# An MLP block in fast matrix products: factors, copies, looks and sums of x take other engines and other places

## The chip, the cores and the metric

The kernel runs on one core of a Trainium2 chip. A core has five engines that work side by side, each through its own queue of instructions in order: TensorE (PE; its weight loads are PEld), VectorE (DVE), ScalarE (ACT), GpSimd (POOL) and SyncE (SP), which here only issues transfers. Sixteen DMA engines move data. The metric is device time in microseconds (us) of one execution.

## The reference

```python
def reference(x, w1, w2):          # x: 8 x 1024 x 1024, w1: 1024 x 4096, w2: 4096 x 1024
    h = x @ w1
    h = 0.5 * h * (1 + np.tanh(np.sqrt(2 / np.pi) * (h + 0.044715 * h ** 3)))
    return (h @ w2).astype(np.float32)
```

There are 8192 rows of x: two large products with a gelu between them.

## The kernel before, in words

Both products are done with fewer multiplications than the plain way. The first takes x and w1 as 2x2 blocks and forms seven products of sums of blocks instead of eight; the second uses a larger scheme of 26 products (`PRODUCTS`). The sums are made by VectorE in f16. To keep f16 in range, rows of x and column groups of w1 are scaled: a "look" finds the size of a tile, its reciprocal scales the cast to f16, and the factors `us` and `rs` undo and redo the scaling at the gelu.

**Tiles.** x comes in 64 chunks of 128 rows (`c`), two to an index `k` (32 of them). w1 is handled in four column groups `r`. A *unit* `u` is one pair (k, r), 128 in all, in the list `order`: first the six first k for r = 0 to 3 (24 units), then each middle k with its four r (a *quad* of units), then the last four k for each r. The first six units (`Plain`) use plain products, because the sums are not ready yet; the rest (`Quad1`) use the seven.

**A unit of Quad1.** `unit(u)` (L662) writes out, in order, m1 of the new unit, m7 of the unit before, the gelus g21 (of two units before) and g11, m3, m2, m6, the gelus g22 and g12, m5, m4, with slots 0 to 6 between them. m1, m6, m7 and m4 add to one PSUM bank `pa`; after m1 (L446), m6 (L456) and m7 (L465) ScalarE copies the bank out, and the next product into the same bank must wait for that copy. VectorE adds the other banks to these copies (L159). A gelu (L397) writes `e`, GpSimd scales and casts it to `g` (L168), and SyncE stores `g` in DRAM (`gd`, L402). Stores are held back a little by `let_go`.

**Order.** Nothing is scheduled automatically: each engine runs its instructions as they are written out. Side work is put into slots by `plan(u, slot, ...)`, `early(p, ...)` (step p of the first 24, four steps to a Plain unit) and done by `background`. Side work is: loading x (L177), the look (`look_x`, L181, a pass of ScalarE over the chunk that leaves a sum), `scale_x` (L184, L188, VectorE), the cast to f16 (L170), turning it (`turn_x_pe`: TensorE and a copy from PSUM, L213 on ScalarE or L215 on VectorE; later by a transposing DMA, L199), the four sums of x (`sum_x`, L159 and L162, tiles `xs`), the looks at w1 (L143), its scale (L262: `rows` on TensorE, L153, spreads the largest value), its casts and its sums (T1, T3, T2, T4), and, from about 390 to 660 us, loading, casting (`wu`) and summing (`wt`) w2, whose loads also go through SyncE's queue.

**Start.** Two chunks of x are loaded, looked at, cast and turned; a warm-up of 56 matmuls that compute nothing (L362) follows on TensorE, while VectorE takes the eight looks at w1. `factors(k, r)` (L229) makes `us` and its reciprocal `rs` with three VectorE instructions.

**Later x.** For a quad that starts at unit a, chunk h of x is loaded in slot 5 of unit a-7+h (L625), looked at in slot 5 of a-6+h (L626), cast in slot 4 and turned in slot 6 of a-5+h; its sums come in slot 5 of a-2 (L629).

Of the kernel before, what the change touches and what calls it, by code (L numbers as in the profile page):

```python
# [9 lines left out]
F16 = mybir.dt.float16  # L10
ACT = mybir.ActivationFunctionType
ALU = mybir.AluOpType
AX = mybir.AxisListType
P = 128
TINY = 1e-18
# [60 lines left out]
def kernel(  # L76
# [17 lines left out]
    HK = H // P // 2  # L94
    IK = I // P // 2
    NP = T // (2 * P)
    NR = I // 2 // N
# [8 lines left out]
    k4 = ctx.enter_context(tc.tile_pool(name="k4", bufs=15))  # L106
# [10 lines left out]
    xl = small.tile([P, T // P], F32, name="xl")  # L117
    xm = small.tile([P, T // P], F32, name="xm")
    xi = small.tile([P, T // P], F32, name="xi")
# [4 lines left out]
    w1m = small.tile([P, NR], F32, name="w1m")  # L124
    w1i = small.tile([P, NR], F32, name="w1i")
# [6 lines left out]
    us = small.tile([P, NP, 2, NR], F32, name="us")  # L132
    rs = small.tile([P, NP, 2, NR], F32, name="rs")
# [6 lines left out]
    V, S, G = nc.vector, nc.scalar, nc.gpsimd  # L140

    def absmax(dst, src):
        V.tensor_reduce(  # L143
            out=dst, in_=src, op=ALU.max, axis=AX.X, apply_absolute_value=True
        )
# [12 lines left out]
    def add(o, a, b):  # L158
        V.tensor_tensor(out=o, in0=a, in1=b, op=ALU.add)  # L159

    def sub(o, a, b):
        V.tensor_tensor(out=o, in0=a, in1=b, op=ALU.subtract)  # L162

    def cast(eng, o, i, s):
        if eng is S:
            S.activation(out=o, in_=i, func=ACT.Copy, scale=s)  # L166
        elif eng is G:
            G.tensor_scalar(out=o, in0=i, scalar1=s, scalar2=1.0, op0=ALU.mult, op1=ALU.mult)  # L168
        else:
            V.tensor_scalar(out=o, in0=i, scalar1=s, scalar2=None, op0=ALU.mult)  # L170


    xraw, x16, xT, xset = {}, {}, {}, {}

    def load_x(c, pool=k4, tag="k4"):
        xraw[c] = pool.tile([P, H], F32, name="xn", tag=tag)
        nc.sync.dma_start(out=xraw[c], in_=x2[c * P:(c + 1) * P, :])  # L177

    def look_x(c):
        junk = k2.tile([P, H], mybir.dt.bfloat16, name="junk", tag="k2")  # L180
        S.activation(out=junk, in_=xraw[c], func=ACT.Abs, accum_out=xl[:, c:c + 1])  # L181

    def scale_x(c):
        V.tensor_scalar(  # L184
            out=xm[:, c:c + 1], in0=xl[:, c:c + 1], scalar1=2.0 ** -13, scalar2=TINY,
            op0=ALU.mult, op1=ALU.max,
        )
        V.reciprocal(xi[:, c:c + 1], xm[:, c:c + 1])  # L188

    def cast_x(c, eng):  # L190
        scale_x(c)
        x16[c] = k2.tile([P, H], F16, name="x16", tag="k2")
        cast(eng, x16[c], xraw.pop(c), xi[:, c:c + 1])

# [19 lines left out]
        else:  # L214
            V.tensor_copy(out=xT[k][:, c % 2], in_=turned)  # L215

    def sum_x(k):
        t = xT[k]
        s = k4.tile([P, 4, HK, P], F16, name="xs", tag="k4")
        sums(s, t[:, 0, 0:HK], t[:, 0, HK:], t[:, 1, 0:HK], t[:, 1, HK:])  # L220
        xset[k] = s

    def sums(s, a11, a12, a21, a22):
        add(s[:, 1], a21, a22)
        sub(s[:, 2], s[:, 1], a11)
        sub(s[:, 3], a11, a21)
        sub(s[:, 0], a12, s[:, 2])

    def factors(k, r):  # L229
        at = slice(r, r + 1) if r is not None else slice(0, NR)  # L230
        for h in range(2):
            V.tensor_scalar(
                out=us[:, k, h, at], in0=w1m[:, at],
                scalar1=xm[:, 2 * k + h:2 * k + h + 1], scalar2=None, op0=ALU.mult,
            )
        V.reciprocal(rs[:, k, :, at], us[:, k, :, at])


    BLOCKS = (B11, B21, B12, B22)
# [3 lines left out]
    def load_w1(r, n, pool=wpool, tag="w"):  # L243
        b, half = BLOCKS[n // 2], n % 2
        row = (b in (B21, B22)) * HK * P + half * 2 * P
        col = (b in (B12, B22)) * I // 2 + r * N
        wraw[r, n] = pool.tile([P, 2, N], F32, name="wn", tag=tag)
        (G if r else nc.sync).dma_start(
            out=wraw[r, n],
            in_=w1[row:row + 2 * P, col:col + N].rearrange("(c p) n -> p c n", p=P),  # L250
        )

    def look_w1(r, n, keep):
        absmax(w1c[:, r, n:n + 1], wraw[r, n].rearrange("p c n -> p (c n)"))
        if not keep:
            wraw.pop((r, n))
# [10 lines left out]
    def cast_w1(r, n, eng):  # L267
        b, half = BLOCKS[n // 2], n % 2
        if (r, b) not in w1set:
            w1set[r, b] = wpool.tile([P, HK, N], F16, name="w", tag="w")  # L270
        cast(eng, w1set[r, b][:, 2 * half:2 * half + 2], wraw.pop((r, n)), w1i[:, r:r + 1])
# [87 lines left out]
    def warm_up(t, n):  # L359
        warm = bank("pb")  # L360
        for _ in range(n):
            nc.tensor.matmul(  # L362
                warm[:, :N // 2], lhsT=t[:, :P], rhs=t[:, :N // 2],
                start=True, stop=True, skip_group_check=True,
            )
# [196 lines left out]
    at = {}  # L562
# [5 lines left out]
    def plan(u, slot, f, *args):  # L568
        assert 0 <= u, (f, args)
        todo.setdefault((u, slot), []).append((f, args))  # L570

    def background(u, slot):
        for f, args in todo.pop((u, slot), ()):
            f(*args)


    def early(p, f, *args):
        plan(p // 4, p % 4, f, *args)

    for k in range(1, FIRST):  # L580
        for h in range(2):
            c = 2 * k + h
            if k > 1:
                p = (3, 7, 11, 14)[k - 2] + h
                early(p, look_x, c)
                early(p, cast_x, c, V)
            if k > 3:
                early((2, 5)[k - 4], load_x, c, wpool, "w")
            early(4 * k - 2 + 2 * h, turn_x_pe, c, V)
    for k in first:  # L590
        plan(*((4, 0), (4, 2), (5, 0), (5, 3), (FIRST, 3), (FIRST + 2, 3))[k], sum_x, k)
        for r in range(1, NR):
# [5 lines left out]
    early(16, widest_w1, 1)  # L598
    early(18, scale_w1, 1)
    for n in range(8):  # L600
        early(19 + n // 2, cast_w1, 1, n, (V, S, G, V, S, V, G, V)[n])
    for i, t in enumerate((T1, T3, T2, T4)):
        plan(5, (2, 3, 3, 3)[i], sum_w1, 1, t)
    for r in range(2, NR):
# [15 lines left out]
    for k in list(middle) + list(last):  # L620
        a = at[k] if k in middle else at[last[0]]
        for h in range(2):
            c = 2 * k + h
            late = 0 if k in middle else 2 * (k - last[0]) - 4
            plan(a - 7 + late + h if k in middle else a - 8 + late, 5, load_x, c)  # L625
            plan(a - 6 + late + h, 5, look_x, c)  # L626
            plan(a - 5 + late + h, 4, cast_x, c, V)
            plan(a - 5 + late + h, 6, turn_x, c, nc.sync)
        plan(a - 2 + late, 5, sum_x, k)  # L629
        plan(a - 2 + late, 4, factors, k, None)  # L630

    u = at[middle[0]] - 1
# [21 lines left out]
    for i, node in enumerate(FORMS):  # L654
        r, n = divmod(i, 7)
# [46 lines left out]
    with tc.manual_schedule(  # L702
        engines={
            mybir.EngineType.PE, mybir.EngineType.Activation, mybir.EngineType.DVE,
            mybir.EngineType.Pool, mybir.EngineType.SP,
        }
    ):
        for c in range(2):
            load_x(c, wpool, "w")
        for n in range(8):  # L710
            load_w1(0, n)
        V.memset(ones, 1.0)
        make_identity(nc, identity)
        V.tensor_copy(out=identity16, in_=identity)
        for c in range(2, 8):
            load_x(c, wpool, "w")
        for c in range(2):
            look_x(c)
            cast_x(c, S)
            t = x16[c]  # L720
            turn_x_pe(c, S)
        warm_up(t, WARM)
        for n in range(8):
            look_w1(0, n, True)
        widest_w1(0)
        scale_w1(0)
        warm_up(t, 16)
        for n in (0, 1, 2, 3, 4, 5):
            cast_w1(0, n, S if n in (2, 3) else V)
        factors(0, 0)  # L730
        for c in (2, 3):
            look_x(c)
        for c in (2, 3):
            cast_w1(0, c + 4, V)
            cast_x(c, V)
        factors(1, 0)
        for k in range(FIRST):
            if k > 1:
                factors(k, 0)
            Plain(k, 0).run(  # L740
                ("pa", "pc", "pa", "pc"),
                lambda i: [background(k, j) for j in ((i,) if i < 3 else (3, 4, 5, 6))],
            )
        now = {}
        for u in range(FIRST, NQ):
            unit(u, None)
        V.tensor_scalar(out=vo, in0=xm, scalar1=w2n, scalar2=None, op0=ALU.mult)
        V.tensor_scalar(out=vn, in0=vo, scalar1=-1.0, scalar2=None, op0=ALU.mult)
        for u in range(NQ, NQ + 2):
            unit(u, lambda i: second(3))  # L750
        let_go()
        for u in range(NQ + 2, NQ + 6):
            for slot in range(7):
                background(u, slot)
        assert not todo, todo.keys()
        second(NP * len(PRODUCTS) - done[0])
# [28 lines left out]
```

## Time and profile before

| what | value |
|---|---|
| median of 3 runs | 1564.81 us (1564.51 to 1565.39) |
| the profiled execution | 1567.52 us |
| its span in the profile | 1565.5 us |
| granted TensorE clock, mean | 0.998 |
| DMA share, 188 to 400 us | 0.80 |
| DMA share, 400 to 660 us | 0.91 |

By stretch, busy us of each engine (a Quad1 unit without pauses takes 6.04 us):

| stretch (us) | PE | DVE | ACT | POOL |
|---|---|---|---|---|
| 40 to 60 | 16.43 | 16.41 | 10.47 | 9.25 |
| 60 to 80 | 14.91 | 19.09 | 8.05 | 13.11 |
| 80 to 100 | 16.80 | 18.50 | 8.52 | 8.09 |
| 400 to 660 | 254.93 | 209.67 | 195.62 | 151.23 |
| 660 to 828 | 168.00 | 80.46 | 126.30 | 80.19 |

A busy engine isn't the limit by itself; what counts is who waited for whom in a stretch. The time in which TensorE pauses is what a change of side work can reach. In a row of the timeline stand the start, the time taken, the engine, the source line, the operation with its tiles (output before input) and shapes, how many, and in brackets the idle time before and what ended it.

### The profile page before, as it was taken

What the parts mean: (1) busy time and instruction counts of PE and PEld (TensorE: products, weight loads), DVE (VectorE), ACT (ScalarE), POOL (GpSimd) and SP (SyncE); (2) the same over time, 40 slices, a digit from 0 to 9 for tenths busy, and PEclk for the clock granted to TensorE, in tenths of its full rate; (3) what the DMA queues carried; (4) which work ended last, traced back from release to release, by engine and by line L of the source; (5) the groups of instructions that cost most, each with busy time, mean ns of one, the idle gap of its engine ahead of it and who ended that gap; (6) DMA issues with size and microseconds to landing.
All of it is one profiled execution on the core that took longest, in us unless ns stands there. A gap on an engine that the chain in (4) does not pass through costs nothing.

```text
span 1565.5 us, 28636 instructions
## 1 busy us (share of the span) xinstructions
PE 1527.2 (98%) x10437; PEld 1017.8 (65%) x10437; DVE 1189.7 (76%) x2422; ACT 724.5 (46%) x1280; POOL 443.9 (28%) x568
## 2 busy tenths in 40 slices
PE   7889999999999999999999999999999999999999
PEld 4334444444444444444446888888888888888888
DVE  5877766666777787856237888888888888888887
ACT  5457777777777777787663111111111111111111
POOL 2557644444555555655443000000000000000000
PEclk9999999999999999999999999999999999999999
DMA  8545687877899898894589776687677667766863
GB/s 309 168 138 188 183 243 236 245 233 214 250 263 271 235 275 234 276 256 141 184 217 283 140 149 134 123 162 136 137 134 155 138 125 151 143 134 128 162 134 83
DMA packets 459837, 293.92 MB, mean 188 GB/s; under 512 B 333872, under 2 KB 427056, under 8 KB 459696
## 3 DMA queue, kind: packets, MB, share of 16 engines
q1 hardware_dynamic: 456240, 279.52, 71.1%
q0 software_dynamic: 3456, 12.58, 2.5%
q8 instruction: 81, 1.33, 0.4%
q14 instruction: 60, 0.49, 0.1%
HBM read 96.99 MB, written 114.29 MB: 135 GB/s over the span
## 4 chain that ended last, share of the span: by engine, by line
PE 88%; DVE 4%; DMA 4%; ACT 2%; issue 1%; POOL 1%; SPq 0%; ACTq 0%; POOLq 0%; DVEq 0%
PE pa L350 47%; PE pc L350 28%; PE pb L350 13%; DMA wn<-in_w_dram 1%; DMA gd<-g 1%; DVE w1c L143 1%; DMA w<-wd 1%; DVE w L162 1%; ACT e L397 1%; DMA xn<-in_x_dram 1%; DVE e L159 0%; ACT junk L181 0%; DVE xs L162 0%; POOL g L168 0%; ACT w L166 0%
## 5 line engine op out<-in xcount | busy, mean ns | idle before, releaser
L168 POOL TENSOR_SCALAR g<-e,rs 128x512 f16<-128x512 f32 x512 | 396.6, 786 | 372.6 <-ACT e L397 238.3
L350 PEld LDWEIGHTS <-gs 128*128 128x128 f16 x4608 | 450.6, 98 | 55.8 <-DVE gs L162 1.6
L350 PEld LDWEIGHTS <-xs 128*128 128x128 f16 x1952 | 191.1, 98 | 248.0 <-DVE w L162 11.2
L159 DVE TENSOR_TENSOR e<-pc,e 128x512 f32<-128x512 f32 x244 | 160.9, 685 | 194.8 <-ACT e L465 194.3
L350 PEld LDWEIGHTS <-xT 128*128 128x128 f16 x1656 | 161.4, 98 | 198.3 <-DVE xT L215 5.1
L350 PE MATMUL pa<-w,gs 128*128 128x256 f16 x2304 | 288.3, 273 | 1.6 <-ACT e L397 1.0
L350 PE MATMUL pa<-w,xs 128*128 128x512 f16 x976 | 251.3, 380 | 14.7 <-DVE w L162 9.7
L397 ACT ACTIVATE e<-e,us 128x512 f32<-128x512 f32 x366 | 252.8, 722 | 20.1 <-DVE e L159 19.6
L350 PE MATMUL pa<-w,xT 128*128 128x512 f16 x1072 | 253.9, 379 | 4.0 <-DVE xT L215 3.1
L350 PE MATMUL pc<-w,xs 128*128 128x512 f16 x976 | 251.4, 380 | 0.8 <-DVE e L159 0.8
L350 PEld LDWEIGHTS <-gT 128*128 128x128 f16 x2048 | 200.3, 98 | 24.2 <-DMA w<-wd 1.1
L519 ACT ACTIVATE o<-pa,vo 128x256 f32<-128x256 f32 x96 | 45.4, 473 | 335.7 <-PE pa L350 333.3
L350 PE MATMUL pc<-w,gs 128*128 128x256 f16 x1536 | 193.8, 273 | 0.0
L350 PE MATMUL pa<-w,gT 128*128 128x256 f16 x1024 | 132.7, 273 | 0.8 <-DMA w<-wd 0.8
L350 PE MATMUL pb<-w,xT 128*128 128x512 f16 x488 | 125.2, 379 | 0.0
L515 DVE SCALAR_TENSOR_TENSOR o<-pc,vo,o 128x256 f32<-128x256 f32 x160 | 77.1, 482 | 58.4 <-PE pc L350 58.4
L456 ACT COPY e<-pa 128x512 f32<-128x512 f32 x122 | 71.6, 587 | 93.9 <-PE pa L350 89.0
L162 DVE TENSOR_TENSOR gs<-gT,gs 128x1024 f16<-128x1024 f16 x160 | 109.9, 687 | 0.7 <-POOL g L168 0.5
L515 DVE SCALAR_TENSOR_TENSOR o<-pa,vo,o 128x256 f32<-128x256 f32 x192 | 92.4, 481 | 20.1 <-PE pa L350 20.1
L350 PE MATMUL pb<-w,gs 128*128 128x256 f16 x768 | 99.5, 273 | 0.3 <-DMA gd<-g 0.3
L350 PE MATMUL pc<-w,gT 128*128 128x256 f16 x768 | 99.5, 273 | 0.0
L446 ACT COPY e<-pa 128x512 f32<-128x512 f32 x122 | 70.6, 579 | 47.5 <-PE pa L350 47.5
(82 smaller groups left out, 1362.4 us busy)
## 6 DMA issues: line engine op xcount, KB each, us to landing
gd<-g SPq DMA_DIRECT2D x488, 128.0 KB, 2.8
wn<-in_w_dram SPq DMA_DIRECT2D x72, 512.0 KB, 4.7
xn<-in_x_dram SPq DMA_DIRECT2D x64, 512.0 KB, 4.7
out_dram<-o SPq DMA_DIRECT2D x62, 512.0 KB, 3.7
w<-wd SPq DMA_DIRECT2D x25, 512.0 KB, 5.9
wn<-in_w_dram POOLq DMA_DIRECT2D x24, 512.0 KB, 5.4
wd<-wt SPq DMA_DIRECT2D x24, 512.0 KB, 4.4
gd<-g SPq DMA_DIRECT2D x12, 256.0 KB, 4.5
```

The lines of the kernel that those rows point to most:

```text
L143: V.tensor_reduce(out=dst, in_=src, op=ALU.max, axis=AX.X, apply_absolute_value=True)
L159: V.tensor_tensor(out=o, in0=a, in1=b, op=ALU.add)
L162: V.tensor_tensor(out=o, in0=a, in1=b, op=ALU.subtract)
L168: G.tensor_scalar(out=o, in0=i, scalar1=s, scalar2=1.0, op0=ALU.mult, op1=ALU.mult)
L350: nc.tensor.matmul(bank, lhsT=left(i), rhs=right[i], start=start and i == 0, stop=i == n - 1, skip_group_check=True,)
L397: S.activation(out=e, in_=src, func=ACT.Gelu_apprx_tanh, scale=self.u[half])
L446: S.copy(self.e11, self.pa)
L456: S.copy(self.e12, self.pa)
L515: V.scalar_tensor_tensor(out=o, in0=ps, scalar=v, in1=o, op0=ALU.mult, op1=ALU.add)
L519: S.activation(out=o, in_=ps, func=ACT.Copy, scale=v)
```

## The change

1. `factors` goes to GpSimd: for one r, two instructions of 128x2 (`us` = xm times w1m, `rs` = xi times w1i, with no reciprocal); for all r, four of 128x4. In the first units they are written a step after the cast of x.
2. Copies of the turned x for the first half of k = 2 to 5 go from VectorE to ScalarE; the casts of w1's second group (r = 1) are dealt out anew, with one more on ScalarE and one less on VectorE.
3. At the start, three of the eight looks at w1 stand ahead of the second `scale_x` on VectorE.
4. `scale_x` is planned by itself; for middle and last quads the look at x moves from slot 5 to slot 3 of the same unit, the scale stands in slot 4 of the next, before the cast as it did.
5. The four sums of x of those quads go to slots 5 and 6 of unit a-2 and slots 1 and 3 of unit a-1.

```diff
     def cast_x(c, eng):
-        scale_x(c)
         x16[c] = k2.tile([P, H], F16, name="x16", tag="k2")
...
+    def times(o, a, s):
+        G.tensor_scalar(out=o, in0=a, scalar1=s, scalar2=1.0, op0=ALU.mult, op1=ALU.mult)
 
     def factors(k, r):
-        at = slice(r, r + 1) if r is not None else slice(0, NR)
-        for h in range(2):
-            V.tensor_scalar(
-                out=us[:, k, h, at], in0=w1m[:, at],
-                scalar1=xm[:, 2 * k + h:2 * k + h + 1], scalar2=None, op0=ALU.mult,
-            )
-        V.reciprocal(rs[:, k, :, at], us[:, k, :, at])
+        if r is not None:
+            c = slice(2 * k, 2 * k + 2)
+            times(us[:, k, :, r], xm[:, c], w1m[:, r:r + 1])
+            times(rs[:, k, :, r], xi[:, c], w1i[:, r:r + 1])
+        else:
+            for h in range(2):
+                c = 2 * k + h
+                times(us[:, k, h, :], w1m, xm[:, c:c + 1])
+                times(rs[:, k, h, :], w1i, xi[:, c:c + 1])
...
                 early(p, look_x, c)
+                early(p, scale_x, c)
                 early(p, cast_x, c, V)
+                if h:
+                    early(p + 1, factors, k, 0)
...
-            early(4 * k - 2 + 2 * h, turn_x_pe, c, V)
+            early(4 * k - 2 + 2 * h, turn_x_pe, c, V if h or k == 1 else S)
...
-        early(19 + n // 2, cast_w1, 1, n, (V, S, G, V, S, V, G, V)[n])
+        early(19 + n // 2, cast_w1, 1, n, (S, V, G, S, V, S, G, V)[n])
...
-            plan(a - 6 + late + h, 5, look_x, c)
+            plan(a - 6 + late + h, 3, look_x, c)
+            plan(a - 5 + late + h, 4, scale_x, c)
             plan(a - 5 + late + h, 4, cast_x, c, V)
             plan(a - 5 + late + h, 6, turn_x, c, nc.sync)
-        plan(a - 2 + late, 5, sum_x, k)
+        for i in range(4):
+            plan(*((a - 2 + late, 5), (a - 2 + late, 6), (a - 1 + late, 1), (a - 1 + late, 3))[i], sum_x, k, (i,))
         plan(a - 2 + late, 4, factors, k, None)
...
         for c in range(2):
             look_x(c)
+            if c:
+                for n in range(3):
+                    look_w1(0, n, True)
+            scale_x(c)
             cast_x(c, S)
...
         warm_up(t, WARM)
-        for n in range(8):
+        for n in range(3, 8):
             look_w1(0, n, True)
```

`sum_x(k, parts)` now makes the sums named in `parts`. TensorE's and SyncE's queues hold the same instructions in the same order as before.

## The prediction

> **What bounds the kernel now.** The page's busy times come first: TensorE is the engine to fill.
>
> ```profile
> PE 1527.2 (98%) x10437; PEld 1017.8 (65%) x10437; DVE 1189.7 (76%) x2422; ACT 724.5 (46%) x1280; POOL 443.9 (28%) x568
> ```
>
> From 165 to 435 us, from 620 to 825 and from 860 on its matmuls follow each other without a pause, so nothing can be won there; only its pauses elsewhere can be. The table of who waited for whom, for TensorE over the whole span, names them:
>
> ```profile
> PE pa L350 <- DVE w L162: 9.7, 3, 6.2
> PE pa L350 <- ACT e L446: 5.0, 8, 1.2
> PE pa L350 <- DVE xT L215: 3.1, 3, 1.4
> PE rows L153 <- DVE spread L148: 1.8, 2, 1.6
> ```
>
> The three of VectorE lie in the first 161 us. The longest (6.2 us) is where the plain products end: the first quad's matmul with T2 waits for the sums of w1, and the chain of waits shows VectorE working without a break in front of it:
>
> ```profile
> 77.87 1.13 DVE w L162
> 79.00 0.76 DVE xs L159
> ...
> 80.88 2.28 DVE w L162 x2
> ...
> 83.20 1.89 PE pa L350 x4
> ```
>
> The granted clock stands at 0.50 from 80.0 to 86.8 in the windows of this stretch, so the first 8 matmuls after it run at half speed and lose another 1.7 us. The waits for ACT e L446 lie elsewhere: six of the eight, 4.2 us, between 400 and 660, where w2 is cast and summed. One of them, at the timeline's 557 us:
>
> ```profile
> 551.11 0.45 SPq L177 DMA_DIRECT2D xn<-in_x_dram  x1
> 551.72 0.59 ACT L456 COPY e<-pa 128x512 f32<-128x512 f32 x1 [0.38 <-PE pa L350]
> 554.11 1.03 PE L350 MATMUL pa<-w,xs 128*128 128x512 f16 x4
> 556.08 1.06 ACT L181 ACTIVATE junk<-xn 128x1024 bf16<-128x1024 f32 x1 [2.54 <-DMA xn<-in_x_dram]
> 557.14 0.57 ACT L446 COPY e<-pa 128x512 f32<-128x512 f32 x1
> 557.76 1.02 PE L350 MATMUL pa<-w,xs 128*128 128x512 f16 x4 [0.89 <-ACT e L446]
> ```
>
> ScalarE reaches the look at x (L181) 2.5 us before x has landed and stands. Behind it on its queue is the copy of a bank (L446) that TensorE must have before it adds to that bank again. That is the case to learn from, because the change moves this look.
>
> **Part 1, the first looks at w1 (L720 to L728).** Three of eight looks go ahead of the second `scale_x`, into 4.4 us in which VectorE idles. Tiles 0, 1, 2 of w1 land at 7.1, 8.5 and 9.8 us, so the looks run 7.1 to 11.0; the second `scale_x`, ready at 10.5, starts at 11.0. The eighth look then ends near 17.8 rather than 19.8 (its tile lands at 16.6). But these two lines stand between it and the end:
>
> ```profile
> 12.87 7.39 PE L362 MATMUL pb<-x 128*128 128x256 f16 x56
> 20.47 0.30 PE L153 MATMUL rows<-identity,spread 128*128 128x128 f32 x1 [0.21 <-DVE spread L148]
> ```
>
> The warm-up's 56 matmuls are ahead of `rows` on TensorE; they now start 0.6 us later (x is scaled later) and take the same time, so `rows` comes at about 20.7 to 20.8 instead of 20.47. The 2 us are lost behind the warm-up, which is not shortened. **+0.3** (0 to +0.6).
>
> **Part 2, VectorE relieved up to 83 us (factors L229, copies L215, casts L601).** It loses five pairs of factors (0.5 us each: two L232, one L236), four copies of the turned x (0.68 each; on ScalarE a copy is 1.01, L213) and one cast of w1 (0.75): 2.5 + 2.7 + 0.75 = 6.0 us. I walked VectorE's new order with these rows. Up to 60 us each copy of a quad's second half still stands behind a cast that waits for a look on ScalarE, so TensorE's four pauses there shrink from 1.5, 1.5, 1.1 and 0.6 to 1.0, 1.0, 0 and about 1.6: 1.0 won. The moved copies end before TensorE needs them (the first runs 36.4 to 37.4, wanted at 37.7). The spread is ready at 64.1 (65.7 now), w1's reciprocal at 66.3 (68.4 now). Then come sums of x (16 instructions of 0.42, in this stretch 0.42 to 0.72 on average per form), two casts and the sums of w1 at 1.2: T2 is ready at 76.9 with no delays, near 79.4 with the 2.5 us by which the same instructions stretch now beside GpSimd. Taken: 79.5 instead of 83.2, **-3.7** (-2.8 to -5.7), since the rows show the stretching. The half clock costs 1.7 now; the pause falls from 6.2 to about 4.4 us, and pauses of 2.5 us (at 120) did not lower the clock, so I take half: **-0.8** (0 to -1.7).
> The Trainium skill (TensorE: Matmul & The Clock Gate, Part 1) puts the gate's window at about 3.4 us, free-running; by it a pause of 4.4 us may or may not hold one idle window. The granted clock of this trace (64.85 us high, 6.83 low, multiples of 3.41) agrees.
>
> **Part 3, factors on GpSimd (48 instructions of 128x2, 104 of 128x4).** No such instruction is in the trace. Bounds: below 0.10 (its memset of 128x1), above 0.69 (cast of 128x512); the two casts, 0.69 and 1.12 for 512 and 1024 columns, leave 0.27 at no columns, which I take. A pair is 0.54. In units 17 and 23 it stands ahead of GpSimd's last cast of w1 (118.11 and 156.03), for which T3 on VectorE waits: +0.5 at 119; at 156 VectorE starts 0.5 earlier, about 0. **+0.5** (0 to +1.2). Elsewhere GpSimd idles enough (it is 47% busy from 200 to 400): the four of a quad, 1.1 us, hold the next casts of g and the stores behind these on SyncE once in 24 us, and `us` is due two units later.
> [...]
>
> **Part 4, the look at x in slot 3 (L626).** Its load stays in slot 5 of the unit before. In ScalarE's new order the look stands ahead of the unit's copy L456, which TensorE's m7 (L462) waits for, and of two gelus, not behind them. That undoes the pauses in which gelus held the look and the look held L446 (0.45, 0.8, 0.7, 1.05 and 1.3 us at 439, 506, 513, 557 and 614), and about 1.0 of those that wait for VectorE: **-5.3** (-3 to -6.2). Against it stands the load:
>
> ```profile
> DMA to landing us min/median/max: 3.7/3.9/5.4
> ...
> DMA to landing us min/median/max: 4.3/4.8/7.3
> ```
>
> These are x's loads from 200 to 400 and from 425 to 660. In the first stretch nearly all land 0.5 to 1.7 us before the unit's copy L456 starts, and the look slips into ScalarE's 0.8 us of idleness: no loss. In the second, stores that wait for GpSimd hold SyncE's queue, and the landings of the 20 loads lie after the start of that copy by 2.5, 1.6, 0.9, -0.4, 2.7, 2.7, 3.2, 1.6, 1.3, 2.1, 4.3, 0.4, 1.6, 1.7, 2.4, 3.4, 1.2, 2.7, 2.1 and -0.6 us. The copy then starts 1.04 after the landing (556.08 to 557.14). TensorE wants its bank 2.35 us after the copy's usual start (551.72 to 554.11) and can go on 0.62 after the copy's start (557.14 to 557.76), so 1.7 us are free; the pause is landing + 1.04 - 1.72. The same sum for L446 at 557 gives 1.05, as measured. A quad's second load is issued before the first look's pause shows, so that pause is taken off it. Sum: 18.6 us, and 1.0 for the load at 164.2 (1.7 late). Longer units give the DMA engines (0.91 busy from 400 to 660, 0.80 from 200 to 400) more time: at 7% slower their share is 0.86, half way back to 3.9, and the loads of w2 that hold SyncE shorten too. About a third off: **+13** (+3 to +19.6).
>
> **Part 5, sums spread.** The 104 sums of 26 quads keep their number; the last two of four move up to a unit on, and the quad that reads them starts after that: nothing, hidden under the unit's 6.0 us of products; without that cover 0.42 for each late one.
>
> **Sum.** +0.3 - 3.7 - 0.8 + 0.5 - 5.3 + 13 = **+4.0**. The profiled execution took 1567.5 us (its span 1565.5 and 2.0 around), 2.7 over the median of 1564.8; I carry the difference over: 1568.8 by the median.
>
> **Rivals.**
> *The loads come in time* (0.21): SyncE's stores wait for GpSimd's casts, and these for loads of w2; if TensorE's first pauses let that queue clear, later loads land within 0.7 us of the copy and cost nothing. It decides where the landing moves 2 us forward. For it: lateness does not grow along the list. Against: each load of w2 starts the delay afresh. Part 4's 13 falls to 3: -6.0, 1558.8, faster.
> *Half cleared* (0.18): part 4 at 9: 0.0, 1564.8, no change.
> *Nothing cleared, little won early* (0.11): 19.6 in part 4, part 2 at -2.8 and the gate still falling, -4.3 won: +13.3, 1578.
> *The looks don't do what they say*: that the order of w1's looks brings nothing is in the forecast; had the warm-up room, it were -2, inside the range.
> *GpSimd holds VectorE* (0.05): with a sum of 0.42 going to 0.80 at each of some 12 factor instructions up to 83 us, 4.5 us of part 2 are gone: +8.5, 1573.3.
>
> **How the numbers follow.** The forecast has 0.45, from 1566 to 1574. 0.2% is 3.1 us, about what a measurement here tells from no change. Faster: the first rival's 0.20. Same: the second, and 0.07 from the edges of the others, 0.25. Slower: 0.55. The range 1558 to 1577 leaves out some of the third rival and of the first.
>
> **What would show it.** Right: after, L465 copies (the old L456) between 430 and 660 start 1 us after a look whose gap names DMA xn, and TensorE's matmuls on pa wait for that copy, ten times and more; no wait for the copy of m1 there; `rows` at 20.7; TensorE's pause near 77 to 80 us at 3 to 5 us. Wrong: if looks there show no gap for DMA xn, the load came earlier than I think, and the time falls below 1562; if the clock stays at 1.00 and T2 is ready by 77.5, part 2 was worth 7.

## The result, and the profile after

| | us |
|---|---|
| before, median of 5 runs on the same chip | 1565.39 (1564.51 to 1566.96) |
| changed, median of 5 runs | 1580.68 (1579.04 to 1583.88) |
| ratio | 1.0098, 95% interval 1.0084 to 1.0113 |
| profiled execution of the changed kernel | 1581.5, its span 1579.7 (before: 1567.5, 1565.5) |

The change costs 15.3 us (1%), where the prediction had 4.0, and the time lies 3.7 us above its range. The changed file's lines that come up again: L359 is the product (L350 before), L455 the copy of m1 (L446), L465 the copy of m6 (L456), L406 the gelu (L397), L233 the new `times` on GpSimd.

The busy times and TensorE's table of waits in the changed kernel's profile (microseconds in total, times, longest):

```profile
PE 1532.4 (97%) x10437; PEld 1019.2 (65%) x10437; DVE 1165.7 (74%) x2267; ACT 728.6 (46%) x1285; POOL 481.4 (30%) x720
...
PE pa L359 <- ACT e L465: 13.3, 12, 2.4
...
PE pa L359 <- DVE w L162: 9.9, 3, 5.9
PE pb L359 <- DVE gs L162: 2.5, 1, 2.5
```

VectorE is busy 24 us less and GpSimd 37.5 us more, as the diff says; neither is where the time went. The table has a new first line: twelve waits for ScalarE's copy of m6, 13.3 us, where the kernel before had 5.0 us for the copy of m1. The waits for the sums of w1 (9.9 us; 9.7 before) have not shrunk, although VectorE was relieved ahead of them.

What the looks at x (L181) wait for from 165 to 700 us, first before, then changed (microseconds, times):

```profile
  DMA xn<-in_x_dram: 5.2, 5
```

```profile
  DMA xn<-in_x_dram: 34.4, 19
```

ScalarE stood five times in front of a late x, now it stands nineteen times. One of them, in the changed kernel's timeline (start, length, engine, line, and in brackets the idle time before and what ended it):

```profile
553.50 0.75 SPq L177 DMA_DIRECT2D xn<-in_x_dram  x1
...
555.65 1.89 PE L359 MATMUL pa<-w,xT 128*128 128x512 f16 x8
...
558.26 1.06 ACT L181 ACTIVATE junk<-xn 128x1024 bf16<-128x1024 f32 x1 [3.74 <-DMA xn<-in_x_dram]
559.22 0.19 ACT L181 ACTIVATION_READ_ACCUMULATOR junk<-xn 128x1 f32 x1
559.31 0.57 ACT L465 COPY e<-pa 128x512 f32<-128x512 f32 x1
...
559.93 1.02 PE L359 MATMUL pa<-w,xs 128*128 128x512 f16 x4 [2.39 <-ACT e L465]
```

The load is issued at 553.50 and lands some 4.7 us later; the look that waits for it holds ScalarE for 3.74 us; the copy behind it starts 1.05 after the landing (558.26 to 559.31), and TensorE goes on 0.62 after that. These are the steps that the prediction gave, at the same durations (1.04 and 0.62).

To find where the 15 us came from, I took the start of each matmul in the trace, less the start of the one before and the usual distance for its shape, and added up what is left over, half clock included. It gives 35.3 us before and 50.0 after, 14.7 more; the spans differ by 14.2. By stage, with a second profile of the same changed kernel (the last experiment) beside it:

| stage | before | changed | second profile | difference | predicted |
|---|---|---|---|---|---|
| up to 112 us: warm-up, T2's pause, half clock | 20.7 | 20.9 | 20.5 | +0.1, -0.2 | -4.2 |
| 112 to 165 us: later sums of w1 | 4.9 | 5.4 | 5.4 | +0.5, +0.5 | +0.5 |
| 165 to 665 us: looks at x while w2 is cast | 6.2 | 13.4 | 18.5 | +7.2, +12.3 | +7.7 |
| 665 to 700 us: a look at 685, half clock after | 0 | 4.2 | 4.4 | +4.2, +4.4 | 0 |
| from 820 us | 3.5 | 6.2 | 3.9 | +2.7, +0.4 | 0 |

The second profile runs some 5 us behind the first at 660 us; its pause at 666.4 us is the one that the first has at 661.4 and is counted in the same row.

So the prediction's main term has the right mechanism, and in the first profile about the right size (4.6 us more in the second). What failed in both is the start, where 4.2 us were to be won and nothing was, and one late look at 685 us that was not in the sum. The 2.7 us of the last row belong to the first profile alone.

### The profile page after: what moved, and what is told of

Read it like the earlier page. It is cut to its first block, busy times and chain, and to the rows that moved or that the text cites. A ratio compares the mean times of both kernels' runs of the same rounds, so it can differ in the third digit from the quotient of the medians.

```text
span 1579.7 us, 28618 instructions
## 1 busy us (share of the span) xinstructions
PE 1532.4 (97%) x10437; PEld 1019.2 (65%) x10437; DVE 1165.7 (74%) x2267; ACT 728.6 (46%) x1285; POOL 481.4 (30%) x720
## 4 chain that ended last, share of the span: by engine, by line
PE 60%; DMA 2%; ACT 1%; issue 0%; SPq 0%; DVE 0%; POOL 0%; ACTq 0%; POOLq 0%
PE pa L359 31%; PE pc L359 20%; PE pb L359 9%; DMA xn<-in_x_dram 1%; DMA w<-wd 1%; DMA gd<-g 1%; ACT e L465 0%; ACT junk L181 0%; SPq L353 0%; ACT e L406 0%; DVE gs L162 0%; POOL g L168 0%; ACT e L455 0%; DVE o L524 0%; SPq L411 0%
## 5 line engine op out<-in xcount | busy, mean ns | idle before, releaser
L168 POOL TENSOR_SCALAR g<-e,rs 128x512 f16<-128x512 f32 x512 | 386.7, 765 | 337.6 <-ACT e L406 246.1
L359 PEld LDWEIGHTS <-gs 128*128 128x128 f16 x4608 | 450.8, 98 | 56.6 <-DVE gs L162 2.8
L359 PEld LDWEIGHTS <-xs 128*128 128x128 f16 x1952 | 191.7, 98 | 260.3 <-issue 24.5
L359 PEld LDWEIGHTS <-xT 128*128 128x128 f16 x1656 | 161.8, 98 | 197.8 <-DVE xm L184 2.9
L359 PE MATMUL pa<-w,gs 128*128 128x256 f16 x2304 | 288.4, 273 | 0.0
L359 PE MATMUL pa<-w,xs 128*128 128x512 f16 x976 | 253.0, 382 | 24.2 <-ACT e L465 13.3
L359 PE MATMUL pa<-w,xT 128*128 128x512 f16 x1072 | 254.6, 380 | 3.1 <-DVE xm L184 1.9
L406 ACT ACTIVATE e<-e,us 128x512 f32<-128x512 f32 x366 | 252.3, 721 | 9.2 <-DVE e L159 8.8
L359 PE MATMUL pc<-w,xs 128*128 128x512 f16 x976 | 253.1, 382 | 0.0
L359 PEld LDWEIGHTS <-gT 128*128 128x128 f16 x2048 | 200.2, 98 | 24.9 <-DMA w<-wd 1.8
L359 PE MATMUL pc<-w,gs 128*128 128x256 f16 x1536 | 193.8, 273 | 0.2 <-DMA w<-wd 0.2
L359 PE MATMUL pa<-w,gT 128*128 128x256 f16 x1024 | 132.7, 273 | 1.0 <-DMA w<-wd 1.0
L359 PE MATMUL pb<-w,xT 128*128 128x512 f16 x488 | 125.5, 380 | 0.0
L524 DVE SCALAR_TENSOR_TENSOR o<-pa,vo,o 128x256 f32<-128x256 f32 x192 | 92.1, 480 | 19.8 <-PE pa L359 19.4
L359 PE MATMUL pb<-w,gs 128*128 128x256 f16 x768 | 99.5, 273 | 2.5 <-DVE gs L162 2.5
L455 ACT COPY e<-pa 128x512 f32<-128x512 f32 x122 | 71.0, 582 | 66.3 <-PE pa L359 66.0
L465 ACT COPY e<-pa 128x512 f32<-128x512 f32 x122 | 70.7, 580 | 63.8 <-PE pa L359 57.8
L359 PE MATMUL pc<-w,gT 128*128 128x256 f16 x768 | 99.5, 273 | 0.0
```

Of the source, the lines that this page charges most:

```text
L359: nc.tensor.matmul(bank, lhsT=left(i), rhs=right[i], start=start and i == 0, stop=i == n - 1, skip_group_check=True,)
L406: S.activation(out=e, in_=src, func=ACT.Gelu_apprx_tanh, scale=self.u[half])
L455: S.copy(self.e11, self.pa)
L465: S.copy(self.e12, self.pa)
L524: V.scalar_tensor_tensor(out=o, in0=ps, scalar=v, in1=o, op0=ALU.mult, op1=ALU.add)
```

## Experiments

Ratios are to the kernel before on the same chip, with their 95% interval. "Early" in a label means x loaded one unit sooner.

**The look back in slot 5.**

```
-            plan(a - 6 + late + h, 3, look_x, c)
+            plan(a - 6 + late + h, 5, look_x, c)
```

> The changed kernel with only the look at x put back into slot 5 of its unit; all other parts of the change stay. If the look in slot 3 holds the copy e (L465) for an x that has not landed, the pauses 'PE pa L359 <- ACT e L465' (13.3 us, 12 waits) go, the smaller pauses of the kernel before return between 430 and 660 us (about 6 us in place of 13.4), and the 3.9 us at 685 go too: 1580.7 - 7 - 4 = about 1570, and 1567.5 if the pause at 842 was a consequence as well. The rival, that factors on GpSimd or the spread sums cost the time, expects the pauses to stay under other names: 1577 or more.

Measured: 1564.26 us, 0.999 (0.998 to 1.000). All of the loss is gone with this one number. It came out below the 1567.5 to 1570 that I expected: between 165 and 700 us only 2.7 us of pauses are back, not 6. With 6.5 after 820 (eight matmuls at half clock among them) the rest adds up to about that of the kernel before (6.2 and 3.5). The rest of the change (GpSimd's factors, copies on ScalarE, first looks, spread sums) is together worth nothing that can be told from no change.

**Only the look, on the kernel before.** The same line of the kernel before, from 5 to 3.

> The kernel before with only the look at x moved from slot 5 to slot 3. The theory of the late load expects its cost alone: 7 to 11 us over the kernel before, about 1575, with ten or more waits of TensorE for the copy e behind a look that waits for DMA xn between 430 and 690 us. The rival (the loss needs the factors on GpSimd or the spread sums) expects no more than 2 us over the kernel before.

Measured: 1576.08 us, 1.0057 (1.0040 to 1.0074), 9 us slower. Its table of waits has the changed kernel's line:

```profile
PE pa L350 <- ACT e L456: 12.7, 12, 2.1
```

Twelve waits, 12.7 us, with nothing else of the change in the kernel: the look's slot alone makes them. The pause at 685 us (2.31 us) is there as well. The 9 us are what I expected (7 to 11).

**The load a unit earlier, the look in slot 3.**

```
-            plan(a - 7 + late + h if k in middle else a - 8 + late, 5, load_x, c)
+            plan(a - 8 + late + h if k in middle else a - 8 + late, 5, load_x, c)
```

> The changed kernel with the loads of x of the middle quads planned one unit (6 us) earlier, the look still in slot 3. The theory of the late load expects no look between 430 and 660 us to wait for DMA xn by more than 1 us; the 13.4 us of pauses there fall to about 1, and the time to 1580.7 - 12 = about 1568, below 1565 if the pauses at 685 and 842 go with them. The rival expects the loads to wait for a buffer of the pool of 15, so that they land when they did: 1578 to 1582.

Measured: 1560.85 us, 0.9964 (0.9951 to 0.9977): 20 us less than the changed kernel, and 0.4% less than the kernel before. I expected 1568, and below 1565 if the pauses at 685 and 842 us went too; both are absent. No look from 165 to 700 us waits for its load. The pool of 15 gave its buffers a unit sooner without holding SyncE. TensorE's share of the stretch from 425 to 660 us (the columns are the stretch, its length, then busy time and matmuls of each engine, the granted clock, the share of the DMA engines, GB/s), before, changed, and with the early load:

```profile
425.00:660.00 235.00, 229.93 (x1061) 103.68 (x1060) 188.64 (x477) 176.64 (x305) 137.01 (x165) 1.00 0.92 264
```

```profile
425.00:660.00 235.00, 224.44 (x1033) 100.69 (x1032) 177.64 (x433) 169.28 (x293) 142.52 (x196) 1.00 0.88 255
```

```profile
425.00:660.00 235.00, 234.78 (x1087) 106.20 (x1086) 188.27 (x458) 181.49 (x313) 155.75 (x209) 1.00 0.92 266
```

TensorE is idle for 5.1, 10.6 and 0.2 of 235 us. The DMA engines carry more, not less, in the third (0.92 against 0.88): the loads were late because they were issued late.

**The early load on the kernel before**, look still in slot 5: the same edit of the load's line there.

> The kernel before with x of the middle quads loaded one unit earlier and the look in slot 5 as it was. Three of its pauses between 400 and 660 us show the look waiting for the load (at 557 by 2.54 us), the others show gelus ahead of the look. If the late load is what mattered in both kernels, the 6.2 us of pauses fall to 3 or less: 1561 to 1563. The rival, that slot 3 is what wins once the load is early, expects 1564 to 1566.

Measured: 1567.96 us, 1.0014 (1.0004 to 1.0024): no faster, if anything 2 us slower. No look waits for its load here either, but TensorE keeps 5.7 us of pauses between 165 and 665, where the look stands behind two gelus and in front of the copy of m1:

```profile
505.92 0.72 ACT L397 ACTIVATE e<-e,us 128x512 f32<-128x512 f32 x1 [0.97 <-DVE e L159]
506.55 1.04 ACT L181 ACTIVATE junk<-xn 128x1024 bf16<-128x1024 f32 x1
507.49 0.18 ACT L181 ACTIVATION_READ_ACCUMULATOR junk<-xn 128x1 f32 x1
507.58 0.56 ACT L446 COPY e<-pa 128x512 f32<-128x512 f32 x1
```

The gelu waits for VectorE, the look follows it without a gap, and the copy that TensorE needs comes last. My expectation fell; its rival's reason holds in the trace, though its time (1564 to 1566) was missed by 2 us too. The load's lateness is what slot 3 costs, and in the rows above the gelus ahead of the look are what slot 5 costs. With the early load there are 5.7 us of pauses from 165 to 665 in slot 5 and 0.7 in slot 3, but these two kernels also differ in the rest of the change. A run with slot 3 and the early load alone on the kernel before, or with slot 5 and the early load in the changed one, was not made. What the other profiles add: between 165 and 700 us the five with the look in slot 5 have 2.7 to 6.2 us in pauses of over 0.3 us, the six with slot 3 and the early load 0 to 1.0. So slot 3 is the better place once x is there; that it is worth 5 us is not shown, since slot 5 with the late load and the rest of the change had only 2.7.

**The start alone.** Parts 1 and 2 without the factors: the changed kernel with `factors` back on VectorE, the look in slot 5 and the sums together.

> The kernel before with parts 1 and 2 of the change without the factors: three first looks at w1 ahead of the second scale, four copies of the turned x on ScalarE, the casts dealt anew; factors on VectorE, look in slot 5, sums together. By the traces of before and after the start won 1.2 us at the pause and lost 1.1 by five more matmuls at half clock: between -1 and +1 us against the kernel before, the long pause of TensorE still 5.5 to 6.5 us. The prediction's sum, without the factors' share of 2.5 us, expects about -2.

Measured: 1566.67 us, 1.0001 (0.9992 to 1.0011). The long pause ends at 83.18 us (83.20 before).

**The factors alone**, on the kernel before: its `factors` replaced by the changed one with `times`.

> The kernel before with only the factors on GpSimd (part 3). VectorE loses the factor pairs of the first 83 us; the start of the kernel with parts 1 and 2 without them had its long pause end at 83.25 us (before 83.20), with them at 82.00. If the factors' leaving VectorE is what moved it, the pause ends 0.8 to 1.2 us earlier here, and the 0.5 us at 161 are lost: within 1 us of the kernel before. The rival (GpSimd's factors hold VectorE by their shared access) expects the pause's end at 83.2 or later and 2 to 4 us lost overall.

Measured: 1566.43 us, 0.9998 (0.9989 to 1.0008). The time agrees with the first theory, the pause with the rival, whose 2 to 4 us of loss are not there: it ends at 83.25, no earlier than before, although VectorE has lost its factors. Three casts of w1 (L170), 0.75 us each elsewhere, take 5.32 us there (1.95 for two and 1.84 for the third in the kernel before):

```profile
72.59 5.32 DVE L170 TENSOR_SCALAR w<-wn,w1i 128x1024 f16<-128x1024 f32 x3
```

From 73.97 us on GpSimd works through casts and factors there without a break. Since the start itself shifts by up to 1.3 us with the moment at which the clock first rises, I count from the matmul `rows` of w1's first set to the end of the pause: 62.73 us before, 62.46 with the start alone, 62.29 with the factors alone, and 61.01 to 61.04 in the five profiles that have both and nothing else changed up to there. The two halves win 0.3 and 0.4 us by themselves and 1.7 together.

**The seventh cast of w1's second set on ScalarE**, with the early load.

```
-        early(19 + n // 2, cast_w1, 1, n, (S, V, G, S, V, S, G, V)[n])
+        early(19 + n // 2, cast_w1, 1, n, (S, V, G, S, V, S, S, V)[n])
```

> The changed kernel with x loaded one unit earlier and only the seventh cast of w1's second set on ScalarE instead of GpSimd; the order of VectorE's sums stays. If GpSimd's cast (1.11 us), which stands behind its two factors and in front of T2, is what stretches VectorE's first sum of quad 3 from 0.42 to 2.39 us, that sum takes under 1.2 us, T2 comes 1 to 2 us earlier and the long pause is 4 to 5 us instead of 6.1. The rival, that the sum waited for something else, expects 2 us or more for it and the pause unchanged.

Measured: 1562.07 us, 0.9969 (0.9957 to 0.9981). What it is about is this stretch of the changed kernel's timeline:

```profile
75.58 2.39 DVE L159 TENSOR_TENSOR xs<-xT 128x512 f16<-128x512 f16 x1
76.12 0.26 POOL L233 TENSOR_SCALAR us<-xm,w1m 128x2 f32<-128x2 f32 x1
76.36 0.26 POOL L233 TENSOR_SCALAR rs<-xi,w1i 128x2 f32<-128x2 f32 x1
76.59 1.11 POOL L168 TENSOR_SCALAR w<-wn,w1i 128x1024 f16<-128x1024 f32 x1
77.69 0.84 POOL L168 TENSOR_SCALAR g<-e,rs 128x512 f16<-128x512 f32 x1
78.01 0.79 DVE L162 TENSOR_TENSOR xs<-xs,xT 128x512 f16<-128x512 f16 x1
```

A sum of 0.42 us takes 2.39 while GpSimd runs two factors and a cast at their full speed. With the cast away:

```profile
75.82 1.30 DVE L159 TENSOR_TENSOR xs<-xT 128x512 f16<-128x512 f16 x1
```

1.30 us, 1.09 less for a cast of 1.11, and T2's pause falls from 5.93 us of idleness to 4.85. The bound that I had set (under 1.2) was missed by 0.1; the pause is as long as the theory had it. That GpSimd's cast delays VectorE's sum there is shown; what the factors alone do to it (0.26 us each, still beside it in the 1.30) is not told apart. The time is not better by it: the half clock behind the pause is one window shorter, but the later pause at 159 us is 2.03 us here instead of 1.73 and costs eight matmuls at half clock: 1.6 us of pauses and half clock won up to 112 us, 1.4 lost from there to 165.

**T2 first**, with the early load.

```
-        early(19 + n // 2, cast_w1, 1, n, (S, V, G, S, V, S, G, V)[n])
+        early(19 + n // 2, cast_w1, 1, n, (S, V, G, S, V, S, S, V)[n])
...
-        plan(*((4, 0), (4, 2), (5, 0), (5, 3), (FIRST, 3), (FIRST + 2, 3))[k], sum_x, k)
+        plan(*((4, 0), (4, 2), (FIRST, 3), (FIRST + 1, 0), (FIRST + 1, 3), (FIRST + 2, 3))[k], sum_x, k)
...
-    for i, t in enumerate((T1, T3, T2, T4)):
+    for i, t in enumerate((T1, T2, T3, T4)):
         plan(5, (2, 3, 3, 3)[i], sum_w1, 1, t)
```

> The changed kernel with x loaded one unit earlier; on VectorE the sums T1, T2 of w1's second set ahead of T3 and of the sums of quads 2 and 3 (these move into the units after), and the seventh cast of that set on ScalarE, which is idle there, instead of GpSimd. My theory of the 6.1 us pause: TensorE is done with the plain products at 75.4, and T2 comes late because the sums of x stand ahead of it and GpSimd's two factors and its cast hold VectorE's first of them for 2.4 us instead of 0.42. It expects T2 by 77, the pause under 2 us, fewer matmuls at half clock, and a time 4 to 7 us shorter: 1554 to 1557. The rival, that TensorE's own order makes T2 late (VectorE waits 1.55 us at 69 us for the turned x), expects a pause of 4 us or more, 1559 to 1561.

Measured: 1561.78 us, 0.9970 (0.9959 to 0.9981), by its time nearer the rival's case (1559 to 1561); by its trace, the theory's. The long pause and its slow matmuls are gone altogether, and then:

```profile
98.58 2.33 DVE L143 TENSOR_REDUCE w1c<-wn 128x1 f32<-128x1024 f32 x2
100.94 0.16 DVE L268 TENSOR_REDUCE w1a<-w1c 128x1 f32<-128x8 f32 x1
101.14 0.29 DVE L148 TENSOR_SCALAR spread<-ones,w1a 128x128 f32<-128x128 f32 x1
...
101.48 0.33 PE L153 MATMUL rows<-identity,spread 128*128 128x128 f32 x1 [3.23 <-DVE spread L148]
```

TensorE, 6 us further on, meets VectorE's looks at w1's third set, which had been hidden behind the pause: 3.2 us are waited there. A pause at 155.5 us, 2.04 instead of 1.73 long, costs eight matmuls at half clock on top.

**The sums of quads 2 to 5 later**, besides: `sum_x` in slots (FIRST + 1, 3), (FIRST + 2, 3), (FIRST + 3, 5), (FIRST + 4, 5).

> As t2_first_early, with the sums of quads 2 to 5 moved to the units just before those that read them. In t2_first_early the 6.1 us pause was gone, and 3.4 us came back at 98 us, where rows waited for VectorE's looks at w1's third set (VectorE 99% busy from 84 to 100). If VectorE's queue is the bound there, two quads' sums (3.4 us) behind those looks take that wait away: 1557 to 1559. The rival, that the loads of w1 are late there since TensorE runs ahead, expects the wait to stay and 1561.

Measured: 1561.14 us, 0.9968 (0.9955 to 0.9980). The time is the rival's (1561), its reason is not: VectorE works from 88 to 99 us without a gap and never waits for a load of w1, so its queue is the bound there, as I thought. The wait for `rows` falls from 3.2 to 2.2 us, not to nothing, since one quad's sums (89.1 to 92.1 us, one of them 1.94 long) still stand ahead of the last looks. Two windows at half clock, at 116 and 157 us, take the rest.

**The warm-up cut to 36 matmuls**, with the early load: `WARM = 36`.

> The changed kernel with x loaded one unit earlier, and a warm-up of 36 matmuls instead of 56. In that kernel spread is ready at 18.35 us and rows waits until 20.56 behind the warm-up, so the order of the first looks brings nothing. If that is right, rows comes at about 18.5 and everything up to the first pause 2.1 us earlier; the pauses up to 83 us follow TensorE (they wait for VectorE in a chain that starts at rows), so the end comes about 2 us earlier: 1558.8. The rival expects the later loads of w1 or x to take it back: 1560.8 and a longer pause before 60 us.

Measured: 1561.23 us, 0.9960 (0.9947 to 0.9973). `rows` comes 1.1 us earlier (19.44 against 20.56), not 2.1: the second x was turned 0.6 us later in this execution, and the clock rose when less of the warm-up was left. From there to the end of T2's pause it is 61.03 us again, so TensorE keeps the 1.1 us that far; at the end of the trace 0.8 are left. The time, 1558.8 by the theory and 1560.8 by its rival, can't be told from that of the early load alone, 1560.85. That the warm-up hid the first looks at w1 is borne out by half.

**All of it together**: T2 first with the later sums, the warm-up of 36, and T2 ahead of T3 in w1's third and fourth sets too.

> t2_sums_later with the warm-up of 36 matmuls and with T2 ahead of T3 in the later sets of w1 too, where 2.4 and 1.9 us are waited at 119 and 159 us. Expected from the pauses of the early-load kernel: 1.2 us less at each of the two, 2 from the warm-up, 1553 to 1556. The rival: what is won early is waited for later by TensorE (VectorE and the loads of w1 are the bound of the first 160 us), no less than 1558.

Measured: 1552.03 us (1551.01 to 1553.75), 0.9905 (0.9892 to 0.9919): 14.7 us less than the kernel before on the same chip, and more than I expected. Its waits:

```profile
PE rows L153 <- DVE spread L148: 3.5, 2, 2.2
...
PE pa L359 <- DVE w L162: 1.5, 2, 0.9
```

The three waits for the sums of w1 (9.9 us) are down to 1.5, and in the profiled execution the clock stands at 1.00 from the first rise to the end of the kernel. Against the profile without the warm-up's cut and with T2 behind T3 in those sets, whose span is 8.7 us longer: `rows` comes 1.8 us earlier (20 matmuls of 0.107 us would be 2.1), 2.8 us of pauses are gone, and so are 3.4 us for two windows at half clock.

**The sums together again**, in the changed kernel.

> The changed kernel with the four sums and looks of a quad together again in slot 5 (part 5 undone), look still in slot 3. If spreading the sums is free, as predicted: 1579 to 1582, the 13 us of waits for copy e L465 stay. The rival (the spread sums delay the quads' products) expects 1575 or less. It also tells whether the 2.65 us pause at 842 us, which the kernel before with the look in slot 3 lacked, follows from the late looks and GpSimd's factors: if it is there again it does, if not it is an accident of the transfers.

Measured: 1581.45 us, 1.0087 (1.0071 to 1.0103). Spreading the sums costs nothing that can be told. The pause at 842 us is missing (0.36 us there).

**The changed kernel once more.**

> The changed kernel once more, unaltered. Its first profile has a pause of 2.65 us at 842 us followed by eight matmuls at half clock (together 2.7 us more than the kernel before there), which neither the kernel before with the look in slot 3 nor the changed kernel with its sums together showed. If this is an accident of where transfers and stores fall, it is missing here and the time is 1578 to 1580; if it belongs to the change, it is here again at 840 to 846 us and the time 1580 to 1583. The waits behind the looks (13 us between 430 and 690) are expected again in either case.

Measured: 1580.42 us (1578.81 to 1584.37), 1.0088 (1.0055 to 1.0120). The pause at 842 is missing here too: its 2.7 us were an accident of the first profile. But the waits behind looks between 165 and 665 are 18.5 us in this execution, 5 more than in the first, against my expectation of 13; its own time is 1584.37. The size of that term varies from one execution to the next.

## Why the prediction was wrong

**The sign and the main mechanism were right.** Part 4 was to cost 13 for late loads and win 5.3 of old pauses. The runs give both terms: the late load costs 13.4 - 0.7 = 12.7 us in the first profile and 17.8 in the second, and slot 3 wins what slot 5 has more of pauses, 5.0 by the pair compared above and 2 to 6 by the other profiles. "About a third off" for a queue that clears itself has no support: from issue to landing the loads between 425 and 660 us take 4.7 us in the median, and 5.2 in the second profile, 4.8 before, so slower units did not shorten them. That 13 fits the first profile is in part luck, then; why its pauses stay below the whole list's 18.6 us is open, and 18.6 was the nearer value for the second. (One reading is off by little: from 551.72 to 554.11 it is 2.39 us, not 2.35.)

**A look outside the list.** The prediction's list of loads ended at 660 us, where the waits of the kernel before end. At 685 us two looks, of the last middle quad and of the first of the last four, fall into one slot, and in the changed kernel this is SyncE's queue:

```profile
672.02 1.18 SPq L177 DMA_DIRECT2D xn<-in_x_dram  x2
673.30 0.38 SPq L344 DMA_DIRECT2D wd<-wt  x1
673.80 4.43 SPq L198 DMA_TRANSPOSE xT<-x  x1
678.33 2.58 SPq L411 DMA_DIRECT2D gd<-g  x4
681.00 0.40 SPq L177 DMA_DIRECT2D xn<-in_x_dram  x1
```

```profile
685.37 1.06 ACT L181 ACTIVATE junk<-xn 128x1024 bf16<-128x1024 f32 x1 [2.92 <-DMA xn<-in_x_dram]
...
687.47 0.56 ACT L465 COPY e<-pa 128x512 f32<-128x512 f32 x1
...
688.08 1.19 PE L359 MATMUL pa<-w,xs 128*128 128x512 f16 x3 [2.32 <-ACT e L465]
```

The load stands behind a transpose of 4.43 us and four stores, is issued at 681.0 and lands at 685.3; ScalarE waits 2.92 us, does both looks, and the copy comes at 687.47. TensorE's 2.32 us of idleness then lower the clock for eight matmuls. The pause is there in all four profiles with slot 3 and the late load, 2.3 to 2.7 us, with the half clock in three of them; with the early load there is none. The prediction's own sum would have given 0.9 us from the landing in the kernel before (677.57, the copy's start 676.03), and the second look's 1.05 on top: half of it was there to be read. That a pause in this stretch lowers the clock as well was not thought of.

**Part 1, +0.3: right in its mechanism.** The second x is turned 0.6 us later in the first profile, and `rows` comes behind the warm-up at 20.79, though its input is ready at 18.44 (20.47 before; 20.7 to 20.8 predicted). In the second profile it is 21.70, since the clock rises 2 us later there. The 0.3 itself can't be told from such shifts: `rows` comes at 20.39 to 20.96 in the four profiles without this part.

**Part 2, -3.7 and -0.8: wrong, an error as large as the look at 685 us.** T2's pause ends at 81.80 us, not 79.5; counted from `rows`, 1.7 us are won instead of 3.7, and the half clock takes 1.1 of them back. The step that failed is the walk along VectorE's queue, in two places. First, it took VectorE as bound by its own work. In the kernel before, then in the changed one:

```profile
70.09 0.69 DVE L215 COPY xT<-turned 128x1024 f16<-128x1024 f16 x1 [0.50 <-PE turned L208]
...
76.03 1.84 DVE L170 TENSOR_SCALAR w<-wn,w1i 128x1024 f16<-128x1024 f32 x1
```

```profile
69.00 0.69 DVE L214 COPY xT<-turned 128x1024 f16<-128x1024 f16 x1 [1.55 <-PE turned L207]
...
81.80 1.89 PE L359 MATMUL pa<-w,xs 128*128 128x512 f16 x4 [5.94 <-DVE w L162]
```

VectorE waits there for TensorE to turn an x, 1.55 us instead of 0.50, so 1.05 us of the work taken off ahead of that point won nothing there. Second, I had allowed 2.5 us for stretching beside GpSimd. From 60 to 82 us the sums of x (0.42 alone) and the casts of w1 (0.75 alone) take 4.4 us longer than that in the kernel before, 2.7 in the sums and 1.6 in the casts, and 4.7 in the changed one, 4.3 and 0.4. So the 2.5 was about the share of the sums before, left out the casts (the one at 76.03, beside a cast of GpSimd's, takes 1.84), and was 2.2 short. In the changed kernel VectorE's casts are done by 74.5 us, and 2.0 us of stretching fall on the sum at 75.6 instead. The two places together are more than the 2.3 us by which 79.5 was missed; where the walk gave the difference back is not shown. The rival called "GpSimd holds VectorE" (0.05) named the engine, but not the way: it had each of 12 factor instructions stretch a sum, and the whole stretch grew by only 0.3. Nor did the pause shorten where its end moved: TensorE arrives 1.1 us earlier too, and stands idle for 5.94 us (6.24 before). The Trainium skill (GPSIMD Engine Reference, 1. Specifications) says that VectorE's instructions with two SBUF inputs contend with GpSimd for its interfaces to SBUF; the sum of 0.42 us that took 2.39, and 1.30 without the cast, agrees.

**The half clock.** Its length is two windows, 6.83 us, as before; the pause's end, 1.4 us earlier, put more matmuls into it, about 2.7 us lost instead of 1.7. "So I take half" had no ground in the trace: a pause of 4.4 us puts at least 2.2 into one window of 3.413, and by the figures of the last section (an estimate) lowers the clock wherever it falls.

**Part 3, +0.5: right in size, by luck in place.** The pause at 161 us grew by 0.55 (1.90 against 1.35), where the prediction had about 0; at 119 us, where it had 0.5, nothing was lost (2.43 against 2.47). The kernel before with the factors alone on GpSimd has the 161 us pause at 1.91 too, and with the start alone it is 1.34, so the factors are the cause. An instruction of them takes 0.27 us in the median, as estimated (up to 1.79, beside VectorE's sums of w1 at 80 us). **Part 5: right**, the spread sums cost nothing that can be told.

**The rivals.** "Nothing cleared, little won early" (0.11, 1578) comes nearest: the whole lateness, and a clock that still falls. It too counted 2.8 us won in part 2, and no look at 685 us. The loads did not come in time, and the delay did not clear by half; these two had 0.39 together.

## What to carry to other kernels

An instruction that waits for a transfer holds everything behind it on an in-order queue: before moving one forward, move its load forward too, and judge the two together. Here the look alone cost 9 us and the load alone won nothing, and the two together won 5.6 (with the other parts of the change, which by themselves can't be told from no change; the pair alone was not run). Taking work off an engine that is behind wins only up to the next point where it waits for someone (1.05 us were lost so at 69 us); walk the queue to that point before pricing the gain, and expect a removed pause to uncover the wait that it hid (5.9 us removed at 76 us, 3.2 uncovered at 101).

## What the runs showed of the hardware

Whether a pause lowers TensorE's clock depends on where it falls. The clock record changes in steps of 3.413 us. I laid its grid over TensorE's idleness in all fifteen profiles up to 1500 us. Of the windows at full clock, each with more than 2.06 us idle was followed by one at 0.50, and none with less than 1.90 was; 22 fell and 6,455 did not. Between the two values lie 1.90, 2.02, 2.03 and 2.04, which fell, and 1.92 and 2.06, which did not. A pause of 3.23 us, split 1.69 and 1.54 by the grid, did nothing; one of 2.03 inside a window cost eight matmuls, 1.7 us. Once down, the clock came back after each window with 0.13 us idle or less, and stayed down after each with 1.01 or more (the changed kernel's at 82 us among these). The Trainium skill (TensorE: Matmul & The Clock Gate, Part 1) gives a free-running window of about 3.4 us, which these records confirm, but puts the fall behind an idle window; here one that was idle for 60% was enough. Two of the kernel's pauses, at 120 and 159 us, lie at 2.3 and 1.7 to 2.0 us, on the edge; shortening them in the kernel with all of it together won 2.8 us of pause and 3.4 us of clock.
